# Where TensorE's operands start in SBUF: weights' parts 96 bytes into longer slots, the rest at multiples of 128

## The chip, the cores and the metric

The kernel runs on one core of a Trainium2 chip. The metric is device time in microseconds (us) from start to end of one execution; lower is better. The kernel before takes 298.7 us, the median of three runs (298.55 to 298.9). The profile comes from one more execution.

## What is computed

One transformer block on 256 tokens of 1,024 features, all in float32:

```python
u = rms_norm(h, mix_norm_g)
q, k, v, glu_a, glu_g = jnp.split(u @ w_in, splits, axis=-1)      # 512 columns each
attn_out = moba_attention(heads(q), heads(k), heads(v), rel_bias) # 8 heads of 64, causal, one block
conv_out = conformer_conv(glu_a, glu_g, conv_w, conv_b, conv_ln_g, conv_ln_b)  # 31 taps, LayerNorm, silu
h = h + jnp.concatenate([attn_out, conv_out], axis=-1) @ w_out
u = rms_norm(h, ffn_norm_g)
h = h + (jax.nn.silu(u @ w_gate) * (u @ w_up)) @ w_down           # 2,816 wide
return rms_norm(h, final_norm_g)
```

## The kernel before

**Products in three parts.** TensorE multiplies operands of type float32r. To keep float32's precision, each weight tile and each activation tile is split in two: an upper part (`wh`, `uh`), a copy rounded to float32r, and a lower part (`wl`, `ul`), the difference. A product is then three matmuls, wh by uh, wh by ul and wl by uh, added up in PSUM. ScalarE makes the upper parts of the weights and VectorE the lower ones, from raw tiles that SyncE's queue loads. The raw tiles have six slots, `wh` and `wl` nine each, of 128 x 1,024 floats; all weights of the kernel pass through the same slots.

**Two shapes.** A matmul has a stationary operand, 128 columns that a load of weights puts into the array, and a moving operand that streams through. In a and gate (`pa`, `pg`), queries and keys (`pqk`) and the output projection (`py`) the weights' parts are stationary and 256 columns of `u2` (or of the mixed activations `mh`, `ml`) move. In the values (`pv`), gate and up of the feed-forward (both `pf`) and down (`pd`, and `pe` at the very end) it is the other way round: the activations are stationary and 512 columns of weights move (256 in `pe`). A load of weights stands ahead of each matmul. Before this change and after it a and gate have 192 such matmuls, queries and keys 192, output 192, values 48, gate and up 528, down 252 and `pe` 24.

**What sets the order.** `PROGRAM`, a table written out by hand, gives the order of all steps up to the feed-forward; loops give it there. Each engine keeps to the program's order.

**Where the tiles lie.** The pools place their tiles one after another, each rounded up to 32 bytes per partition: first `const`, then `wts` (raw, `wh`, `wl`), then `w1`, which `w2` takes over for the feed-forward. The place where `const` starts is a multiple of 128. In the following a start is given as what is left of the byte address after division by 128. Before, `mhalf` (24 floats, 96 bytes) stands first, so `xs` and `u2` start at 96. `pv` is 16 floats longer than its data, which brings `ones` and `ident` to 0. The sums of squares and small tiles behind them bring `dg`, raw, `wh` and `wl` to 96, and `w2` as well (`fh`, `fl`). In `w1`, `accx` and `rbt` bring what follows to 0, `mh` and `ml` among it. Columns within tiles are cut at multiples of 128 bytes, except in the convolution. The pairs are thus, moving and stationary: a, gate, queries and keys 96 and 96; output 0 and 96; values, feed-forward and `pe` 96 and 96.

Of the kernel before, what the change touches and what calls it, by code (L numbers as in the profile page):

```python
# [10 lines left out]
F32 = mybir.dt.float32  # L11
F32R = mybir.dt.float32r
AF = mybir.ActivationFunctionType
ALU = mybir.AluOpType

P = 128
S = 256
D = 1024
KD = D // P
H = 8  # L20
HD = 64
NB = 32
TAPS = 31
CC = 4
# [6 lines left out]
ZN = 384  # L31
HW = 1024
# [4 lines left out]
FINE = ("a0_0", "a0_4")  # L37
COPY_V = (("a0_0", 0), ("a0_0", 1))
WARM = 9

PROGRAM = """
ld.a1_0 a0.0 pz a0.1 a0.2 a0.3 zs zd ld.a1_1 a0.4 a0.5 a0.6 a0.7 ld.qk0
# [13 lines left out]
PV_N = PV_FOLD + 32  # L56
# [3 lines left out]
def block_kernel(ctx, tc, xT, w_in, w_out, w_gu, w_down, pvec, gfin, relb, hot, out):  # L60
    nc = tc.nc
    const = ctx.enter_context(tc.tile_pool(name="const", bufs=1))
    wts = ctx.enter_context(tc.tile_pool(name="wts", bufs=9))
# [3 lines left out]
    w1 = ph1.enter_context(tc.tile_pool(name="w1", bufs=1))  # L67
# [3 lines left out]
    def mm(*args, **kw):  # L71
        return tc.keep_in_program_order(nc.tensor.matmul(*args, **kw))  # L72
# [12 lines left out]
    act, vec, pool, sync = (InOrder(e) for e in (nc.scalar, nc.vector, nc.gpsimd, nc.sync))  # L85

    def bank(i, name):
        return psum.tile([P, 512], F32, tag=f"b{i}", name=name)
# [17 lines left out]
    def pieces(name):  # L106
        n = HW // 2 if name in FINE else HW
        return [(i, slice(j, j + n)) for i in range(2) for j in range(0, HW, n)]
# [12 lines left out]
    def take(name):  # L121
        if name[0] in "gud" and name not in ("g0", "u0", "g1"):
            while order and len(raws) < 1 + LOOK:
                fetch(order[-1][2])
        return raws.pop(name)
# [5 lines left out]
    def high(name, i):  # L131
        if i == 0:
            raw = take(name)
            upper[name] = []
            parts[name] = []
            for n in range(2):
                wh = wts.tile([P, HW], F32R, tag="wh", name=f"wh_{name}_{n}")
                wl = wts.tile([P, HW], F32R, tag="wl", name=f"wl_{name}_{n}")
                parts[name].append((wh, wl))
                upper[name] += [(raw[n], wh, wl, c) for m, c in pieces(name) if m == n]  # L140
        raw, wh, wl, c = upper[name][i]
        if (name, i) in COPY_V:
            vec.tensor_copy(wh[:, c], raw[:, c])
        else:
            act.copy(wh[:, c], raw[:, c])
        made.add((name, i))
# [3 lines left out]
    def split(name, i=None):  # L150
        for n in range(len(pieces(name))) if i is None else (i,):
            if (name, n) not in made:
                high(name, n)
            raw, wh, wl, c = upper[name][n]
            vec.tensor_sub(wl[:, c], raw[:, c], wh[:, c].bitcast(F32))
# [10 lines left out]

    mhalf = const.tile([P, 24], F32, name="mhalf")
    xs = const.tile([P, KD, S], F32, name="xs")  # L170
    u2 = const.tile([P, KD, 2, S], F32R, name="u2")
    uh, ul = u2[:, :, 0], u2[:, :, 1]
    pv = const.tile([P, PV_N + 16], F32, name="pv")
    ones = const.tile([P, P], F32, name="ones")
    ident = const.tile([P, P], F32, name="ident")
    warm = const.tile([P, 1], F32, name="warm")
    accx = w1.tile([P, S], F32, name="accx")
    rbt = w1.tile([NB + 1, H], F32, name="rbt")
    hot_s = w1.tile([NB + 1, ZN], F32, name="hot_s", tag="lg", bufs=2)
    upad = [w1.tile([P, 2 * UW + 4], F32, name=f"upad{i}", tag="pts", bufs=4) for i in range(2)]  # L180
    ustk = []
    wstk = [w1.tile([P, 8 * Q, 32], F32, name=f"wstk{i}", tag="wstk", bufs=2) for i in range(2)]
    invc = w1.tile([P, P], F32, name="invc")
    vec.memset(warm, 0.0)
    act.dma_start(pv[:, 0:PV_T], pvec[:, 0:PV_T])
    act.activation(warm, warm, AF.Sigmoid)
# [3 lines left out]
        sync.dma_start(xs[:, k], xT[:, k * S : (k + 1) * S])  # L190
    pool.memset(ones, 1.0)
    pool.dma_start(hot_s, hot)
    pool.dma_start(rbt[0:NB, :], relb)
    wm = bank(4, "wm")
    for i in range(WARM):
        mm(wm[:, 0:P], ones, ones, start=i == 0, stop=i == WARM - 1)
    pool.memset(ident, 0.0)
    pool.affine_select(out=ident, in_=ident, compare_op=ALU.not_equal, fill=1.0, base=0,
                       pattern=[[-1, P]], channel_multiplier=1)
    pool.memset(mhalf, -0.5)  # L200
    pool.memset(rbt[NB : NB + 1, :], 1.0)
    for t in upad:
        pool.memset(t[:, 0 : TAPS - 1], 0.0)
        pool.memset(t[:, TAPS - 1 + S : UW + TAPS - 1], 0.0)
        pool.memset(t[:, UW + TAPS - 1 + S :], 0.0)
    pool.memset(invc, 1.0 / (CC * P))
    pool.dma_start(pv[:, PV_T:PV_N], pvec[:, PV_T:])

    col = lambda lo, i: pv[:, lo + i : lo + i + 1]
# [11 lines left out]
    def rstd(acc, n, eps, name, b):  # L221
        ps = bank(b, f"ps_{name}")
        for t in range(2):
            mm(ps[:, t : t + 1], acc[:, t * P : (t + 1) * P], ones[:, 0:1], start=True, stop=True)
        ms = const.tile([P, 2], F32, name=f"ms_{name}")
        vec.tensor_scalar(ms, ps[:, 0:2], 1.0 / n, eps, op0=ALU.mult, op1=ALU.add)
        rc = const.tile([P, 2], F32, name=f"rc_{name}")
        pool.tensor_tensor(rc, ms, mhalf[:, 0:2], op=ALU.pow)
        dg = const.tile([P, S], F32, name=f"dg_{name}", tag="dg")
        for t in range(2):  # L230
            vec.tensor_scalar(dg[:, t * P : (t + 1) * P], ident, rc[:, t : t + 1], None, op0=ALU.mult)
        return rc, dg

    def wide(dg, name, b):
        pb = bank(b, f"pb_{name}")
        mm(pb[:, :S], ones, dg, start=True, stop=True)
        return pb
# [22 lines left out]
    cv = lambda c: cacc[:, c]  # L260
# [75 lines left out]
    def scale_x():  # L336
        xn["c"], xn["d"] = rstd(accx, D, RMS_EPS, "x", 5)
# [16 lines left out]
    pzs = []  # L354

    def bias_mm():
        pzs.append(bank(6, "pz"))
        mm(pzs[0][0:H, 0:ZN], rbt, hot_s, start=True, stop=True)

    def bias_copy():  # L360
        act.copy(zs, pzs[0][0:H, 0:ZN])
# [120 lines left out]
    s4 = w1.tile([P, 2, S], F32, name="s4")  # L482
    ln = {}

    def norm(part):
        if part == 1:
            vec.tensor_add(s4[:, 0], s4[:, 0], s4[:, 1])
        elif part == 2:
            pm = bank(2, "pm")
            mm(pm[:, :S], invc, s4[:, 0], start=True, stop=True)  # L490
            for c in range(CC):
                vec.tensor_sub(cv(c), cv(c), pm[:, :S])
        elif part == 6:
            csq.append(w1.tile([P, CC, S], F32, name="csq", tag="wstk", bufs=2))
            for c in range(CC):
                act.activation(cw(c), cv(c), AF.Square)
        elif part == 3:
            vec.tensor_add(s4[:, 0], cw(0), cw(1))
            vec.tensor_add(s4[:, 1], cw(2), cw(3))
            vec.tensor_add(s4[:, 0], s4[:, 0], s4[:, 1])  # L500
        elif part == 7:
            _, ln["dg"] = rstd(s4[:, 0], CC * P, LN_EPS, "ln", 4)
        elif part == 4:
            ln["r"] = wide(ln["dg"], "ln", 5)
        else:
            for c in range(CC):
                vec.tensor_mul(cv(c), cv(c), ln["r"][:, :S])
                act.activation(cw(c), cv(c), AF.Silu, scale=col(PV_LG, c), bias=col(PV_LB, c))
                act.copy(mix[0][:, 4 + c], cw(c))
            for c in range(CC):  # L510
                vec.tensor_sub(mix[1][:, 4 + c], cw(c), mix[0][:, 4 + c].bitcast(F32))


    acch = const.tile([P, S], F32, name="acch")

    def finish(m):
        assert len(done) == KD - 3
# [7 lines left out]
    def a0(k):  # L525
        high(f"a0_{k // 4 * 4}", k % 4)
        upper_u(k, PV_G1)
        lower_u(k, PV_G1)
        split(f"a0_{k // 4 * 4}", k % 4)
        a_mm(0, k, f"a0_{k // 4 * 4}", k % 4 * 512)  # L530

    ops = {"ld": fetch, "zd": bias_out, "bd": bias_in, "ud": stack_out, "us": stack_in, "h": high, "w": split, "rb": row_scale, "pz": bias_mm, "zs": bias_copy, "vt": v_out, "rs": scale_x,
           "a0": a0, "a1": a1, "glu": glu, "qk": qk_mm, "qo": qk_out, "sc": score, "t": logits, "n": normed, "fl": flip,
           "fo": flip_out, "v": v_mm, "pv": pv_mm, "mo": mix_out, "l": norm, "o": o_mm, "f": finish, "c": conv,
           "co": conv_out, "cw": conv_weights, "ct": conv_taps, "hs": lambda m: sumsq(acch, xs[:, m], m, "h"),
           "sq": lambda k: sumsq(accx, xs[:, k], k, "x"), "g": lambda m: lower_u(m, PV_G2)}
# [96 lines left out]
    for k in range(KD):  # L633
        for t in range(2):
            up_mm(0, t, k)
        if k == 5:
            rc2, _ = rstd(acch, D, RMS_EPS, "h", next(spare))
            split("u1")
# [38 lines left out]
    a, b = FG - 2, FG - 1  # L677
    for t in range(2):
# [22 lines left out]
        ms = w2.tile([P, 2], F32, name=f"fms{t}")  # L701
        for n, (lo, hi) in enumerate(((512, 768), (768, 1024))):
# [5 lines left out]
            if n == 0:  # L708
# [4 lines left out]
                                 op0=ALU.mult, op1=ALU.add, accum_out=ms[:, 1:2])  # L713
# [97 lines left out]
```

## Time and profile before

| | us |
|---|---|
| median of three runs | 298.7 (298.55 to 298.9) |
| the profiled execution | 298.79 |
| its span, first to last instruction | 297.0 |
| TensorE busy with matmuls | 289.4 |
| loads of weights | 246.9 |
| VectorE busy | 203.9 |
| ScalarE busy | 149.7 |
| GpSimd busy | 44.3 |

A matmul's busy time begins when it starts and has a modelled end that overlaps the next one, so the means in the groups of the profile are no price of a matmul. What a matmul costs in a stream is the distance from start to start. The chain of work that ended last, in order of time, shows it directly: it takes each instruction from the end of the one before it, so that a piece's length divided by its count is the distance, apart from what enters at the piece's first instruction.

### The profile page before, as it was taken

To read this page: it belongs to the slowest core of one execution; us is meant where nothing else is said; L and a number is where in the kernel's file an instruction comes from. 1 tells how busy PE (TensorE), PEld (TensorE's weight loads), DVE (VectorE), ACT (ScalarE), POOL (GpSimd) and SP (SyncE) were. 2 spreads that over 40 slices of the span, in tenths; PEclk is the share of its full clock that TensorE was granted. 3 is DMA by queue.
4 is the path that set the end of the run, shared out by engine and by line. 5 is a ranking of instruction groups with operands and counts; after the bars stand their busy time and mean duration, and the time that the engine had idled before them with its cause. 6 is when DMAs were issued, how large, how long until landed. Compare 5 with 4: busy or idle time off the path is not lost.

```text
span 297.0 us, 4763 instructions
## 1 busy us (share of the span) xinstructions
PE 289.4 (97%) x1750; PEld 246.9 (83%) x1750; DVE 203.9 (69%) x373; ACT 149.7 (50%) x251; POOL 44.3 (15%) x83
## 2 busy tenths in 40 slices
PE   8999999999999999999999999999999999999991
PEld 7999986988689998888888888888888888888880
DVE  2877999888988688867875738291847456321884
ACT  2984564354583768826555445271717263402531
POOL 4000000000000000124131303320421313130000
PEclk9999999999999999999999999999999999999996
DMA  6999779936227445797997968979694959520012
GB/s 182 344 406 335 251 170 261 382 94 195 74 73 225 142 144 200 244 354 228 307 348 168 310 166 275 303 259 374 222 282 134 297 144 311 165 71 0 1 68 75
DMA packets 21624, 63.73 MB, mean 215 GB/s; under 512 B 3117, under 2 KB 5701, under 8 KB 21600
## 3 DMA queue, kind: packets, MB, share of 16 engines
q1 hardware_dynamic: 18176, 54.80, 57.2%
q0 software_dynamic: 2992, 8.08, 9.8%
q10 hardware_dynamic: 432, 0.54, 0.5%
q8 instruction: 14, 0.23, 0.3%
q14 instruction: 10, 0.08, 0.1%
HBM read 58.08 MB, written 5.32 MB: 213 GB/s over the span
## 4 chain that ended last, share of the span: by engine, by line
PE 92%; issue 2%; DMA 2%; DVE 1%; SPq 0%; POOLq 0%; POOL 0%; ACT 0%; DVEq 0%
PE pf L72 40%; PE pd L72 17%; PE pqk L72 8%; PE py L72 8%; PE pv L72 4%; PE pa L72 4%; PE pg L72 4%; PE pc L72 4%; DMA xs<-in_xT 2%; PE ps L72 1%; PE pt L75 1%; PE po L72 1%; DVE ht L83 1%; SPq L83 0%; DVE hg L83 0%
## 5 line engine op out<-in xcount | busy, mean ns | idle before, releaser
L72 PE MATMUL pf<-wh_u,u 128*128 128x512 f32 x176 | 56.2, 390 | 0.0
L72 PE MATMUL pf<-wh_g,u 128*128 128x512 f32 x176 | 55.9, 389 | 0.0
L83 DVE TENSOR_TENSOR ff<-fs,pf 128x256 f32<-128x256 f32 x22 | 9.1, 420 | 53.4 <-ACT fs L83 53.4
L83 ACT ACTIVATE fs<-pf,rc_h 128x256 f32<-128x256 f32 x22 | 10.4, 476 | 65.9 <-PE pf L72 65.4
L72 PEld LDWEIGHTS pf<-wh_u,u 128*128 128x128 f32 x176 | 33.0, 188 | 6.8
L72 PEld LDWEIGHTS pf<-wh_g,u 128*128 128x128 f32 x176 | 33.0, 188 | 6.8
L72 PE MATMUL pf<-wl_g,u 128*128 128x512 f32 x88 | 34.2, 389 | 0.0
L72 PE MATMUL pf<-wl_u,u 128*128 128x512 f32 x88 | 34.2, 389 | 0.0
L72 PE MATMUL pd<-wh_d,fh 128*128 128x512 f32 x84 | 32.9, 391 | 0.0
L72 PE MATMUL pd<-wh_d,fl 128*128 128x512 f32 x84 | 32.7, 390 | 0.0
L72 PE MATMUL pd<-wl_d,fh 128*128 128x512 f32 x84 | 32.7, 389 | 0.0
L83 DVE TENSOR_TENSOR wl_u<-raw_u,wh_u 128x1024 fp32r<-128x1024 f32 x22 | 26.6, 1223 | 7.5 <-ACT wh_u L83 7.4
L83 POOL DMA_DIRECT2D fb<-fd x40 | 23.2, 588 | 46.5 <-DMA fd<-fv 22.8
L83 ACT CAST wh_u<-raw_u 128x1024 fp32r<-128x1024 f32 x22 | 22.9, 1053 | 12.5 <-PE pf L72 9.2
L83 DVE TENSOR_TENSOR wl_g<-raw_g,wh_g 128x1024 fp32r<-128x1024 f32 x22 | 25.9, 1221 | 2.0 <-ACT wh_g L83 2.0
L83 DVE TENSOR_TENSOR wl_d<-raw_d,wh_d 128x1024 fp32r<-128x1024 f32 x22 | 25.6, 1205 | 0.5 <-ACT wh_d L83 0.5
L72 PE MATMUL pqk<-u,wh_qk 128*128 128x256 f32 x128 | 23.6, 286 | 0.0
L83 ACT CAST wh_g<-raw_g 128x1024 fp32r<-128x1024 f32 x22 | 22.0, 1049 | 0.0
L83 ACT CAST wh_d<-raw_d 128x1024 fp32r<-128x1024 f32 x22 | 21.9, 1045 | 0.0
L72 PEld LDWEIGHTS pqk<-u,wh_qk 128*128 128x128 f32 x128 | 20.0, 192 | 0.4 <-issue 0.3
L72 PEld LDWEIGHTS pf<-wl_u,u 128*128 128x128 f32 x88 | 16.5, 188 | 3.4
L72 PEld LDWEIGHTS pf<-wl_g,u 128*128 128x128 f32 x88 | 16.5, 188 | 3.4
(156 smaller groups left out, 558.4 us busy)
## 6 DMA issues: line engine op xcount, KB each, us to landing
raw_g<-in_w_gu SPq DMA_DIRECT2D x22, 512.0 KB, 5.6
raw_u<-in_w_gu SPq DMA_DIRECT2D x22, 512.0 KB, 7.0
raw_d<-in_w_down SPq DMA_DIRECT2D x22, 512.0 KB, 4.7
raw_qk<-in_w_in SPq DMA_DIRECT2D x8, 512.0 KB, 7.2
raw_o<-in_w_out SPq DMA_DIRECT2D x8, 512.0 KB, 4.2
fd<-fv POOLq DMA_DIRECT2D x10, 256.0 KB, 4.0
fb<-fd POOLq DMA_DIRECT2D x40, 64.0 KB, 5.8
ustk<-ud SPq DMA_DIRECT2D x8, 288.0 KB, 5.7
```

The source lines that it names most:

```text
L72: return tc.keep_in_program_order(nc.tensor.matmul(*args, **kw))
L75: return tc.keep_in_program_order(nc.tensor.transpose(o, i, ident))
L83: return lambda *a, **k: tc.keep_in_program_order(f(*a, **k))
```

## The change

The tiles are placed anew; no instruction is moved. The row of instructions of each engine is the same in order, with three differences: GpSimd's `memset` of `invc` is gone, the mean of the convolution's LayerNorm is a product with `ones` where it was one with `invc` (whose elements were 1/512), and VectorE's four subtractions of it are multiply-and-adds that bring in the -1/512.

- `wh` and `wl` have slots of 1,056 floats. The weights of a and gate (`a0`, `a1`), queries and keys (`qk`) and output (`o`) begin 24 floats into them; those of values, gate, up and down at the slot's start.
- `mhalf` stands behind `ident` and has 2 floats, `pv` is 8 floats shorter, and one tile `acc` in `const` serves as `accx` and as `acch`. `xs`, `u2`, `dg`, raw and the slots of `wh` and `wl` start at 0.
- `rbt` is 32 floats wide, of which 8 are used. `w1` and `w2` start at 0, and `mh`, `ml`, `fh` and `fl` lie at 0.

The pairs, moving and stationary, are now: a, gate, queries and keys 0 and 96; output 0 and 96, as before; values, feed-forward and `pe` 0 and 0.

```diff
+SHIFT = {"a": 24, "q": 24, "o": 24}
...
             for n in range(2):
-                wh = wts.tile([P, HW], F32R, tag="wh", name=f"wh_{name}_{n}")
-                wl = wts.tile([P, HW], F32R, tag="wl", name=f"wl_{name}_{n}")
+                s = SHIFT.get(name[0], 0)
+                wh, wl = (wts.tile([P, HW + 32], F32R, tag=w, name=f"{w}_{name}_{n}")[:, s : s + HW] for w in ("wh", "wl"))
                 parts[name].append((wh, wl))
...
-    mhalf = const.tile([P, 24], F32, name="mhalf")
+
     xs = const.tile([P, KD, S], F32, name="xs")
     u2 = const.tile([P, KD, 2, S], F32R, name="u2")
     uh, ul = u2[:, :, 0], u2[:, :, 1]
-    pv = const.tile([P, PV_N + 16], F32, name="pv")
+    pv = const.tile([P, PV_N + 8], F32, name="pv")
     ones = const.tile([P, P], F32, name="ones")
     ident = const.tile([P, P], F32, name="ident")
+    mhalf = const.tile([P, 2], F32, name="mhalf")
     warm = const.tile([P, 1], F32, name="warm")
-    accx = w1.tile([P, S], F32, name="accx")
-    rbt = w1.tile([NB + 1, H], F32, name="rbt")
+    accx = acch = const.tile([P, S], F32, name="acc")
+    rbt = w1.tile([NB + 1, 32], F32, name="rbt")
...
-    invc = w1.tile([P, P], F32, name="invc")
...
-    pool.memset(invc, 1.0 / (CC * P))
...
-            mm(pm[:, :S], invc, s4[:, 0], start=True, stop=True)
+            mm(pm[:, :S], ones, s4[:, 0], start=True, stop=True)
             for c in range(CC):
-                vec.tensor_sub(cv(c), cv(c), pm[:, :S])
+                vec.scalar_tensor_tensor(cv(c), pm[:, :S], -1.0 / (CC * P), cv(c), op0=ALU.mult, op1=ALU.add)
...
-    acch = const.tile([P, S], F32, name="acch")
```

## Rows read from the trace of the kernel before

**Rows 1.** The page: busy engines, TensorE's granted clock in 40 slices, chain by engine.

```profile
PE 289.4 (97%) x1750; PEld 246.9 (83%) x1750; DVE 203.9 (69%) x373; ACT 149.7 (50%) x251; POOL 44.3 (15%) x83
...
PEclk9999999999999999999999999999999999999996
...
PE 92%; issue 2%; DMA 2%; DVE 1%; SPq 0%; POOLq 0%; POOL 0%; ACT 0%; DVEq 0%
```

**Rows 2.** Waits of TensorE's weight loads, the longest: us in total, times, longest.

```profile
PEld wm L72 <- POOL ones L83: 1.0, 1, 1.0
PEld pa L72 <- ACT u L83: 0.8, 1, 0.8
PEld ps L72 <- DVE cacc L83: 0.8, 2, 0.4
```

**Rows 3.** The chain in order of time: start, length (us), engine, tile, line, count.

```profile
18.52 0.24 PE pg L72 x2
18.75 0.24 PE pa L72 x2
...
30.91 8.64 PE pqk L72 x72
...
54.11 2.88 PE pqk L72 x24
...
95.51 14.24 PE py L72 x120
...
142.91 5.44 PE pd L72 x24
148.35 10.88 PE pf L72 x48
```

**Rows 4.** Groups by shape, TensorE: count, busy us, mean ns, then idle before.

```profile
L72 PE MATMUL pf<-wh_g,u 128*128 128x512 f32 x176 | 55.9, 389 | 0.0
...
L72 PE MATMUL pd<-wh_d,fh 128*128 128x512 f32 x84 | 32.9, 391 | 0.0
...
L72 PE MATMUL pqk<-u,wh_qk 128*128 128x256 f32 x128 | 23.6, 286 | 0.0
...
L72 PE MATMUL pa<-u,wh_a 128*128 128x256 f32 x64 | 13.7, 295 | 0.1
...
L72 PE MATMUL pv<-wh_v,u 128*128 128x512 f32 x32 | 10.8, 399 | 0.0
```

**Rows 5.** Timeline of TensorE's matmuls, us 118.4 to 121, first and last rows.

```profile
118.45 0.39 PE L72 MATMUL pf<-wl_u,u 128*128 128x512 f32 x1
118.68 0.63 PE L72 MATMUL pf<-wh_u,u 128*128 128x512 f32 x2
...
120.53 0.39 PE L72 MATMUL pf<-wl_u,u 128*128 128x512 f32 x1
120.76 0.39 PE L72 MATMUL pf<-wh_u,u 128*128 128x512 f32 x1
```

**Rows 6.** Groups by shape, loads of float32 stationary operands that start at 0, 96 and 32.

```profile
L72 PEld LDWEIGHTS ps_ln<-ones,s 128*128 128x128 f32 x4 | 0.5, 190 | 0.0
L72 PEld LDWEIGHTS ps_x<-ones,accx 128*128 128x128 f32 x4 | 0.5, 190 | 0.2 <-DVE accx L83 0.2
L72 PEld LDWEIGHTS ps_h<-ones,acch 128*128 128x128 f32 x4 | 0.5, 190 | 0.2 <-DVE acch L83 0.2
```

**Rows 7.** Groups by shape, VectorE and GpSimd, around the LayerNorm's mean.

```profile
L83 DVE SCALAR_TENSOR_TENSOR ht<-pe,rc_h,ht 128x256 f32<-128x256 f32 x4 | 1.9, 483 | 0.2
...
L83 DVE TENSOR_TENSOR cacc<-cacc,pm 128x256 f32<-128x256 f32 x4 | 1.4, 417 | 0.2 <-PE pm L72 0.2
...
L83 POOL MEMSET invc<- 128x128 f32 x1 | 0.2, 210 | 0.0
```

**Rows 8.** Timeline of VectorE behind the mean's subtraction.

```profile
83.18 1.42 DVE L83 TENSOR_TENSOR cacc<-cacc,pm 128x256 f32<-128x256 f32 x4 [0.19 <-PE pm L72]
84.51 0.96 DVE L83 TENSOR_TENSOR ml<-po,mh 128x256 fp32r<-128x256 f32 x2
86.54 0.76 DVE L83 TENSOR_TENSOR ml<-po,mh 128x256 fp32r<-128x256 f32 x2 [1.07 <-ACT mh L83]
```

More of the change, by code (lines that the diff above doesn't have):

```diff
@@ L192, in block_kernel @@
     pool.dma_start(hot_s, hot)
-    pool.dma_start(rbt[0:NB, :], relb)
+    pool.dma_start(rbt[0:NB, 0:H], relb)
     wm = bank(4, "wm")
@@ L200, in block_kernel @@
     pool.memset(mhalf, -0.5)
-    pool.memset(rbt[NB : NB + 1, :], 1.0)
+    pool.memset(rbt[NB : NB + 1, 0:H], 1.0)
     for t in upad:
@@ L227, in rstd @@
         rc = const.tile([P, 2], F32, name=f"rc_{name}")
-        pool.tensor_tensor(rc, ms, mhalf[:, 0:2], op=ALU.pow)
+        pool.tensor_tensor(rc, ms, mhalf, op=ALU.pow)
         dg = const.tile([P, S], F32, name=f"dg_{name}", tag="dg")
@@ L357, in bias_mm @@
         pzs.append(bank(6, "pz"))
-        mm(pzs[0][0:H, 0:ZN], rbt, hot_s, start=True, stop=True)
+        mm(pzs[0][0:H, 0:ZN], rbt[:, 0:H], hot_s, start=True, stop=True)
     def bias_copy():
```

## The prediction, made before the result was seen

> **What bounds the kernel now.** The page comes first: TensorE is busy for 289.4 of 297.0 us, 92% of the chain that ended last lies on it, and its granted clock is at the upper of its two levels, 2.4 GHz, in every slice but the last, where it has no more matmuls [rows 1]. Then its waits: the loads of weights ahead of the matmuls stand still for 1.0 us at the very start, 0.8 us once more in the start for `u`, and 0.8 us in two pieces later [rows 2]. So the time is the number of matmuls times their distance, and every nanosecond per matmul is seen in the end, with nothing else late. That is why the chain in order of time is the view to read [rows 3]; busy means such as 286 or 389 ns [rows 4] contain modelled ends and are no distances.
>
> The distances fall into three classes, and here the start of the operands comes in.
> - 256 columns, moving at 96, stationary at 96: queries and keys take 8.64 us for 72, which is 120.0 ns; a burst of 24 takes 2.88 us, again 120.0; a and gate take 0.24 us for two [rows 3].
> - 256 columns, moving at 0, stationary at 96: output takes 14.24 us for 120, which is 118.67 ns [rows 3]. It is the only float32r stream of the kernel with different starts, and it is 1.33 ns faster although it does the same work.
> - 512 columns, 96 and 96: gate and up take 10.88 us for 48, down 5.44 us for 24, both 226.67 ns [rows 3].
>
> The step from 256 to 512 columns at 96 and 96 is 106.67 ns, exactly 256 columns at 2.4 GHz. What is left over, 13.33 ns, is the same for both widths, so it is a price per matmul and not per column, and it is the thing that a start could change. It is not always 13.33: behind an interruption 512-column matmuls are slower for a while. From 118.45 to 120.53 us stand nine distances (the rows with x2 hold two) in 2.08 us, 231.1 ns each, before the stream settles at the 226.67 that the long pieces show [rows 5, 3]. Which distance a stream settles at is therefore a state, and the change moves operands, so it can move that state in either direction.
>
> **The change part by part.**
>
> Queries, keys, a and gate go from 96 and 96 to 0 and 96, which is what output has. There are 192 + 192 matmuls; the first 24 of a and gate run in the start, where they wait for transfers, so 360 count. At the output's distance each saves 1.33 ns, 0.48 us in all; some fifty of them stand right behind interruptions, where the streams have not settled, and I take 0.45 us. Bounds: nothing if the output's 1.33 ns come from something else in that stream (0 us), and the whole 13.33 ns if the left-over went entirely (360 x 13.33 ns = 4.8 us). I take the output's value since it is the same width, type and pair of starts.
>
> Values, gate and up, and down go from 96 and 96 to 0 and 0: 48 + 528 + 252 = 828 matmuls of 512 columns, and 24 of 256 in `pe`. No float32r row has 0 and 0. The float32 loads whose stationary operand starts at 0, 96 and 32 take 190 ns each [rows 6], so the start of a stationary operand by itself costs nothing there; what distinguishes the output from queries and keys is then either the moving start alone or the difference of the two starts. By the difference, 0 and 0 is the same as 96 and 96 and nothing happens. By the moving start alone, each of the 828 saves what the output saves, 1.33 ns, 1.10 us in all. From above: the settled state is lost, and each stays at the 231.1 ns of rows 5, 4.44 ns more; about 60 of them are in that state anyway, so 765 x 4.44 ns = 3.4 us dearer. From below: the whole left-over goes, 828 x 13.33 ns = 11.0 us. I take zero, by the difference: the nearest row is gate and up itself, whose operands keep their position against each other.
>
> The mean of the LayerNorm: four multiply-and-adds on VectorE in place of four subtractions. One with an input in PSUM takes 483 ns against 417 [rows 7], together 0.26 us more. Behind them VectorE makes `ml` from 84.51 us and then idles 1.07 us, waiting for ScalarE [rows 8]; that idle time takes the 0.26 us in, and TensorE's waits name nothing there [rows 2]. Cost nothing; without the cover 0.26 us. The removed `memset` (0.21 us [rows 7]) was GpSimd's and nobody waited for it. `acc` as one tile makes the second sum of squares wait for reads of the first, which belongs to the start of the kernel: nothing.
>
> The transfers write raw tiles and `xs` at 0 instead of 96. In the start alone is anybody waiting for them, 0.8 us [rows 2]. No row has the same transfer at another start; it is worth at most those 0.8 us, as much the other way, and I take zero. Writes of VectorE and ScalarE at another start: no row shows a price, TensorE never waits for them in the feed-forward, zero.
>
> Sum: 297.0 - 0.45 = 296.55 us of span. The profiled execution has 1.79 us around its span (298.79) and lies 0.09 us over the median of the runs, so the time is 298.25, in round numbers **298.3 us**.
>
> **The rivals.**
>
> *The wide matmuls gain too (faster).* The moving start alone counts, and the 828 go at 1.33 ns less: 298.25 - 1.10 = 297.15 us. For it: output and queries differ in exactly that start. Against it: they differ in the difference as well. Its far end, with all 13.33 ns gone from the 828, is 287.2 us; against this end speaks that output, whose moving operand starts at 0 already, still pays 12.0 ns of the 13.33.
>
> The Trainium skill's "TensorE: Matmul & The Clock Gate", under "Back-to-back issue gap", gives N / 2.4 + 2.5 ns for a warm matmul alone, which would be 109 and 216 ns here, an estimate from that page. The trace disagrees at every start it has: 118.67, 120.0 and 226.67 [rows 3].
>
> *The settled state is lost (slower).* At 0 and 0 the wide streams stay at the distance they have behind an interruption, 231.1 ns. It decides from the first long piece of gate and up; the time is 298.25 + 3.4 = 301.65 us. For it: the slower state exists, in each burst behind an interruption [rows 5], and moving the operands helped output precisely by keeping it out of a settled 120.0; the same can happen to a stream that is better off settled. Against it: the two starts keep their difference.
>
> *Starts do nothing (no change).* What makes output faster is something else, its four banks or the place of `mh`, and all starts are alike: 298.7 us. For it: the float32 loads don't care [rows 6]. Against it: output is the one stream with another pair, and the one with another distance.
>
> The Trainium skill speaks for this rival: "SBUF — State Buffer", under "Specifications (TRN2)", has lines of 16 bytes, and 0 and 96 are both multiples of 16, so a read touches as many lines from either; its "Operand start alignment" says that its rule is about legality, not speed. The output's 118.67 against 120.0 [rows 3] is not explained by it.
>
> **How the numbers follow.** The forecast has 0.42, the wide gain 0.28 (of which 0.08 for ends well below 297), the lost state 0.18, no effect 0.12. The forecast's own range is 297.6 to 298.9 us, by the transfers of the start and by some 60 unsettled matmuls of 512 columns that may settle sooner or later (60 x 4.44 ns = 0.27 us). To hold 8 in 10 the range takes in the wide gain at 297.15 and the lost state at 301.65: 296.6 to 301.9 us; the far end of the gain is left out. A measurement of this kernel tells 0.2% (0.6 us) from no change. Below 298.1 lie the wide gain and about a quarter of the forecast's chance: faster 0.38. Within 0.2% lie the rest of the forecast and no effect: 0.43. Slower by more is the lost state and a little of the rest: 0.19.
>
> **What the profile after would show.** In the chain: queries and keys at about 118.7 ns (72 in 8.54 us), output unchanged, gate and up at 226.67 (48 in 10.88 us). Queries and keys at 120.0 would make the first term wrong; 48 of gate and up in 10.82 us or less would show the wide gain, in 11.09 the lost state. Any wait of TensorE's loads over 1 us outside the start would mean that I overlooked who becomes late.

## The result: slower, and only from the feed-forward on

The changed kernel takes 301.43 us (median, 301.04 to 302.82) where the kernel before took 298.8 us in the same session (298.55 to 299.65). The ratio is 1.0092, 95% interval 1.0066 to 1.0119. The forecast was 298.3 us; the time is that of the rival "the settled state is lost", which gave 301.65 us.

The page of the changed kernel, as in rows 1 (busy engines, granted clock in 40 slices, chain by engine):

```profile
span 299.3 us, 4761 instructions
...
PE 291.4 (97%) x1750; PEld 245.8 (82%) x1750; DVE 204.0 (68%) x373; ACT 149.1 (50%) x251; POOL 44.0 (15%) x82
...
PEclk9999999999999999999999999999999999999997
...
PE 92%; issue 2%; DMA 2%; DVE 1%; SPq 0%; POOLq 0%; POOL 0%; ACT 0%; DVEq 0%
```

TensorE bounds the kernel as before, at the upper of its two clock levels in all but the last slice. So the clock does not explain the loss, and neither does a new wait: the longest waits of the weight loads are those of rows 2, within 0.2 us.

```profile
PEld pa L74 <- ACT u L85: 1.0, 1, 1.0
...
PEld ps L74 <- DVE cacc L85: 0.8, 2, 0.4
```

The chain in order of time, to be read against rows 3 (start, length in us, engine, tile, line, count):

```profile
30.07 8.52 PE pqk L74 x72
...
53.06 2.81 PE pqk L74 x24
...
94.29 14.28 PE py L74 x120
108.57 8.31 PE pf L74 x36
117.22 25.04 PE pf L74 x108
142.27 5.58 PE pd L74 x24
147.85 11.11 PE pf L74 x48
158.95 5.57 PE pd L74 x24
164.52 11.09 PE pf L74 x48
...
258.95 5.57 PE pd L74 x24
```

Queries and keys fell from 120.0 to 118.3 ns (8.52 us for 72). Gate and up rose from 226.67 to 231.0-231.5 ns (11.09 or 11.11 us for 48), down to 232 (5.57 for 24). From 142.27 to 258.95 us lie seven rounds of 72 wide matmuls: 116.68 us for 504, 231.5 ns each.

The balance: the last piece of output ended at 95.51 + 14.24 = 109.75 us before [rows 3]; now the feed-forward begins at 108.57, 1.18 us earlier. The span ends 2.3 us later (299.3 against 297.0). So 3.48 us went in the feed-forward and behind it, 4.46 ns for each of its 780 wide matmuls. That they are unsettled, and not evenly slower, is seen in the timeline of single matmuls (start, busy us): the starts lie 0.23, 0.23, 0.24 and 0.23 us apart.

```profile
195.82 0.40 PE L74 MATMUL pd<-wl_d,fh 128*128 128x512 f32 x1
196.05 0.39 PE L74 MATMUL pd<-wh_d,fl 128*128 128x512 f32 x1
196.28 0.40 PE L74 MATMUL pd<-wh_d,fh 128*128 128x512 f32 x1
196.52 0.40 PE L74 MATMUL pd<-wl_d,fh 128*128 128x512 f32 x1
196.75 0.39 PE L74 MATMUL pd<-wh_d,fl 128*128 128x512 f32 x1
```

In the trace's nanoseconds such a stretch repeats distances of 230, 236 and 234. Elsewhere, as at the end of the piece from 181.15 to 192.27 us, there are runs of six or seven at 226 and 227: the stream finds the settled distance and loses it again. What the two stretches have different is said behind the second experiment.

### The profile page after: what moved, and what is told of

Same layout as the page of the kernel before. It is cut to its first block, busy times and chain, and to the rows that moved or that the text cites. A ratio compares the mean times of both kernels' runs of the same rounds, so it can differ in the third digit from the quotient of the medians.

```text
span 299.3 us, 4761 instructions
## 1 busy us (share of the span) xinstructions
PE 291.4 (97%) x1750; PEld 245.8 (82%) x1750; DVE 204.0 (68%) x373; ACT 149.1 (50%) x251; POOL 44.0 (15%) x82
## 4 chain that ended last, share of the span: by engine, by line
PE 92%; issue 2%; DMA 2%; DVE 1%; SPq 0%; POOLq 0%; POOL 0%; ACT 0%; DVEq 0%
PE pf L74 41%; PE pd L74 18%; PE py L74 8%; PE pqk L74 8%; PE pv L74 4%; PE pa L74 4%; PE pc L74 4%; PE pg L74 4%; DMA xs<-in_xT 2%; PE ps L74 1%; PE pt L77 1%; PE po L74 1%; DVE ht L85 1%; SPq L85 0%; DVE hg L85 0%
## 5 line engine op out<-in xcount | busy, mean ns | idle before, releaser
L74 PE MATMUL pf<-wh_u,u 128*128 128x512 f32 x176 | 56.9, 393 | 0.0
L74 PE MATMUL pf<-wh_g,u 128*128 128x512 f32 x176 | 56.7, 393 | 0.0
L74 PEld LDWEIGHTS pf<-wl_g,u 128*128 128x128 f32 x88 | 16.5, 188 | 3.7
L74 PEld LDWEIGHTS pf<-wl_u,u 128*128 128x128 f32 x88 | 16.5, 188 | 3.7
```

## The experiments

In the words of the sections ahead a start was what is left of an address after division by 128. That is too coarse here. From the built programs I took, for every float32r matmul, the **difference**: start of the moving operand less start of the stationary one, what is left after division by 256. Before, gate, up, down, values, queries, keys, a and gate had 0, and output 160. In the changed kernel a slot of 1,056 floats is 4,224 bytes, 16.5 times 256, so that neighbouring slots lie 128 apart in this measure. Feed-forward: 408 matmuls at 0 and 372 at 128. A, gate, queries, keys and output: mixed, 32 and 160.

**Every pair of starts, streams alone.** No transformer: bursts of 48 matmuls, wide then narrow (512 and 256 columns), float32r, a load of weights ahead of each, all 16 pairs of starts of 0, 32, 64 and 96 bytes, slots of 4,096.

```python
for m, s in PAIRS:          # floats: 0, 8, 16, 24 for moving and stationary
    rest(g)                 # two small float32 products
    wide(m, s, g)
...
```

> This kernel leaves the transformer out: it runs only TensorE streams of 48 float32r matmuls, first 16 of 512 moving columns, then 16 of 256, one for each pair of starts (moving, stationary) out of 0, 32, 64 and 96 bytes past a multiple of 128, with two small float32 matmuls between the streams, and copies an input to the output. Operand sequences are those of gate and up (wide) and of queries and keys (narrow); slots of weights are 4,096 bytes apart, and no other engine works meanwhile. Theory 'start': where the operands start within 128 bytes decides by itself; then the wide stream at (96, 96) settles at 226.7 ns and that at (0, 0) stays near 231.5 ns, as in the two traces. Theory 'slots': the 4,224-byte distance of the slots unsettles the streams, so that here, with 4,096, (0, 0) and (96, 96) both settle at 226.7. Theory 'difference' (that of the prediction): equal differences of the starts give equal distances, all four equal pairs alike. For the narrow streams: (96, 96) 120.0 and (0, 96) 118.7 by all three.

Measured distance in ns, mean of the last 24 of each burst, by difference. Pairs with the same difference agree within 0.05 ns, whatever the starts themselves.

| difference | 0 | 32 | 64 | 96 | -32 | -64 | -96 |
|---|---|---|---|---|---|---|---|
| wide | 226.67 | 233.33 | 228.88 | 233.33 | 233.33 | 233.33 | 234.17 |
| narrow | 120.0 | 116.67 | 117.75 | 120.0 | 118.33 | 117.75 | 117.38 |

0 and 0 is indeed the same as 96 and 96: neither operand's start counts by itself. And the two widths want different things: zero is the best of these for wide matmuls and the worst for narrow ones.

**Every difference in steps of 16.** The same streams, stationary operand at 0, moving one at 0 to 240 bytes.

```diff
-PAIRS = [(m, s) for m in (0, 8, 16, 24) for s in (0, 8, 16, 24)]
+PAIRS = [(m, 0) for m in range(0, 64, 4)]
```

> Again streams alone, without the transformer: the stationary operand starts at a multiple of 256, the moving one 0, 16, 32 and so on to 240 bytes past a multiple of 256, 48 matmuls of 512 columns and then 48 of 256 for each; slots 4,096 bytes apart. Theory 'difference within 256': the distance goes by the difference of the two starts modulo 256. Then wide: 226.67 ns at 0, about 228.9 at 64, 233 to 234 at 32, 96, 160, 192 and 224, as in the streams before, and over 230 at 128, which has the same start modulo 128 as 0. Narrow: 120.0 at 0, 116.7 at 32, 117.75 at 64 and 192, 118.3 at 224. Theory 'difference within 128': 128 is the same as 0 in both, 226.67 and 120.0, and the loss with longer slots has another cause.

| difference | 0 | 16 | 32 | 48 | 64 | 80 | 96 | 112 |
|---|---|---|---|---|---|---|---|---|
| wide | 226.67 | 231.67 | 233.33 | 233.33 | 228.88 | 231.08 | 233.33 | 226.67 |
| narrow | 120.0 | 118.71 | 116.67 | 118.33 | 117.75 | 120.0 | 120.0 | 113.33 |

| difference | 128 | 144 | 160 | 176 | 192 | 208 | 224 | 240 |
|---|---|---|---|---|---|---|---|---|
| wide | 232.08 | 233.33 | 234.17 | 233.33 | 233.33 | 234.58 | 233.33 | 236.67 |
| narrow | 118.83 | 118.54 | 117.42 | 119.21 | 113.33 | 119.17 | 118.33 | 116.92 |

128 is not 0: nearly half of the changed kernel's wide matmuls have it, and a stream of it alone goes at 232.08 ns. That is not the whole loss. If the others had kept 226.67 ns, 372 x 5.41 ns = 2.0 us would be lost, and 3.48 are. With each start of the trace set beside its matmul's difference, the matmuls at 0 are seen to lose as much: interruptions left out, the next start follows after 231.1 ns on average behind a matmul of the feed-forward at 0 and after 231.6 behind one at 128. The repeated 236, 234 and 230 ns above go with differences that repeat 0, 128, 0: 236 from 0 to 128, 234 from 128 to 0, 230 from 0 to 0. The seven distances of 226 and 227 before 192.1 us lie behind seven matmuls at 0, which follow five more at 0. This speaks for the change of difference from one matmul to the next keeping a stream unsettled, at 0 too; a stream that alternates was not run alone.

The timeline gives whole bursts, here for wide at 0, 112 and 128 and for narrow at 0 and 112 (start, us from the first start to the last end, count):

```profile
9.97 11.52 PE L28 MATMUL b<-w,u 128*128 128x512 f32 x48
...
91.19 11.13 PE L28 MATMUL b<-w,u 128*128 128x512 f32 x48
...
102.52 11.40 PE L28 MATMUL b<-w,u 128*128 128x512 f32 x48
...
195.87 6.00 PE L28 MATMUL b<-u,w 128*128 128x256 f32 x48
...
238.91 5.74 PE L28 MATMUL b<-u,w 128*128 128x256 f32 x48
```

At 0 the wide burst is the longest of the three, 11.52 us, but that is no price of 0: it is the first burst of the kernel, with two long distances at its start (573 and 356 ns), and from the fourth distance on it goes at 226.67. In the run before, the later bursts at 0 take 11.13 to 11.18 us and settle after one to ten matmuls; at 112 it is one, and the same distance. At 128 the burst does not settle within its 48. One point disagrees with the run before: narrow at 192 (-64) gave 113.33 here and 117.75 there, so what a narrow stream settles at also depends on how it came in.

**The long slots alone.** The kernel before, with slots of 1,056 floats, every part at its slot's start, and, for room, the shared `acc` and the mean by `ones`. All starts are as before modulo 128.

```diff
-                wh = wts.tile([P, HW], F32R, tag="wh", name=f"wh_{name}_{n}")
-                wl = wts.tile([P, HW], F32R, tag="wl", name=f"wl_{name}_{n}")
+                wh = wts.tile([P, HW + 32], F32R, tag="wh", name=f"wh_{name}_{n}")[:, 0:HW]
+                wl = wts.tile([P, HW + 32], F32R, tag="wl", name=f"wl_{name}_{n}")[:, 0:HW]
...
```

> The kernel before with slots of 1,056 floats for the weights' parts, but every part still at the slot's start, so that all pairs of starts modulo 128 are those of the kernel before (the shared accumulator and the product with ones come along, to make room). Theory 'start': the streams of 512 columns keep 226.67 ns, 48 of gate and up in 10.88 us, time 298.8 us, ratio 1.000. Theory 'slots': they go to about 231.5 ns as in the changed kernel, 48 in 11.1 us, and without the gain of queries and keys the time is about 302 us, ratio 1.011.

302.42 us, ratio 1.0114 (1.0088 to 1.0139). Its chain shows the changed kernel's pieces:

```profile
143.68 5.58 PE pd L72 x24
149.25 11.11 PE pf L72 x48
160.36 5.57 PE pd L72 x24
165.93 11.09 PE pf L72 x48
```

5.58, 11.11, 5.57, 11.09: to the digit what the changed kernel has, though here u and the weights stand where they stood modulo 128. From the start of the feed-forward's first matmul to that of the last (`pe`) it is 184.0 us in both kernels, against 180.6 before. The length of the slots makes the loss, with no shift of any part.

**No shift, short slots.** The changed kernel with slots of 1,024 floats and nothing shifted, so that u, `mh` and all weights have difference 0. Everything else of the change stays.

```diff
-SHIFT = {"a": 24, "q": 24, "o": 24}
+SHIFT = {}
...
-... wts.tile([P, HW + 32], F32R, tag=w, name=f"{w}_{name}_{n}")[:, s : s + HW] ...
+... wts.tile([P, HW], F32R, tag=w, name=f"{w}_{name}_{n}")[:, s : s + HW] ...
```

> The changed kernel with slots of 1,024 floats and no shift, so that every float32r operand starts at a multiple of 128 and slots are 4,096 bytes apart. Theory 'start': the wide streams, at 0 and 0, stay near 231.5 ns (48 of gate and up in 11.1 us), time 301.5 us or a little more, ratio 1.009 to 1.012, according to what the narrow ones do at 0 and 0. Theory 'slots' and theory 'difference': 226.67 ns, narrow ones at 120.0 as at 96 and 96, output at 120.0 too, time 299.0 us, ratio 1.001.

299.17 us, ratio 1.0008 (0.9988 to 1.0028).

```profile
30.73 8.64 PE pqk L74 x72
...
95.32 14.38 PE py L74 x120
...
142.87 5.44 PE pd L74 x24
148.31 10.88 PE pf L74 x48
```

The loss is gone: 226.67 ns for wide, at starts of 0 modulo 128, and 180.6 us from the feed-forward's first matmul to the last. So are the gains: queries and keys are back at 120.0, and output, now at difference 0 too, rose from 14.24 to 14.38 us and settles at 120.0. The output's 1.33 ns before were its difference of 160, not its moving start. The rest of the change (the mean by multiply-and-add, the one `acc`, transfers to other starts) costs nothing that can be seen.

**u moved alone.** The kernel before with `mhalf` behind `u2` instead of ahead of it, which puts `xs` and `u2` 96 bytes lower. Difference of the feed-forward's gate and up and of the values 96, of a, gate, queries and keys 160, of down 0 as before.

```diff
-    mhalf = const.tile([P, 24], F32, name="mhalf")
     u2 = const.tile([P, KD, 2, S], F32R, name="u2")
+    mhalf = const.tile([P, 24], F32, name="mhalf")
```

> The kernel before with one line moved: the 24 floats of mhalf stand behind xs and u2 instead of ahead of them. u2 then starts at 0 and everything behind it stays at 96: a, gate, queries and keys 0 and 96, values and gate and up 96 and 0, down 96 and 96 as before; slots 4,096 bytes apart. Theory 'start', if the moving operand's start is what counts: the wide streams stay at 226.67 ns, a, gate, queries and keys gain 1.33 ns each, time 298.35 us, ratio 0.9985. Theory 'start', if the stationary operand's counts: gate and up 231.5 ns, 528 x 4.8 ns = 2.5 us, time 300.9, ratio 1.007, down unchanged at 226.67. Theory 'difference': gate and up lose their settled state as their difference changes, 300.9 us as well; theory 'slots': 298.35 us.

302.34 us, ratio 1.0116 (1.0091 to 1.0141).

```profile
143.62 5.47 PE pd L72 x24
149.09 11.20 PE pf L72 x48
```

Gate and up: 11.20 us for 48, 233.3 ns, the streams' value for 96. Down, in the same kernel, settles at 226.67 within each 24 (5.47 us, 0.03 for the way there). The weights are in the same slots in both, and of the operands of TensorE's float32r matmuls only u has moved, which is gate and up's stationary operand: the moving start alone cannot be what counts. The theory 'difference' had the direction, and 300.9 us was too low, because it took 231.5 ns for a difference that costs 233.3: 528 x 6.67 ns is 3.5 us and not 2.5.

**Only the narrow matmuls off zero.** The kernel before with u 32 bytes further until the feed-forward, and `accx` 32 floats longer, which moves `mh` and `ml`. Differences: a, gate, queries, keys and output 32, feed-forward 0.

```diff
-    u2 = const.tile([P, KD, 2, S], F32R, name="u2")
+    u2 = const.tile([P, KD * 2 * S + 64], F32R, name="u2")
+    at = lambda lo: u2[:, lo : lo + KD * 2 * S].rearrange("p (k l s) -> p k l s", k=KD, l=2)
+    u_in, u_ff = at(8), at(0)
...
-    accx = w1.tile([P, S], F32, name="accx")
+    accx = w1.tile([P, S + 32], F32, name="accx")[:, 0:S]
...
```

> The kernel before with its slots; u2 is 64 floats longer, and before the feed-forward its data lie 8 floats further in (a difference of 32 for a, gate, queries and keys, and of 224 for values), in the feed-forward at the start (difference 0); the sum of squares is 32 floats longer, which brings mh and ml to a difference of 32 too. Theory 'difference within 256', by the streams alone: narrow matmuls at 116.67 ns, 360 x 3.33 = 1.2 us less for a, gate, queries and keys, 192 x 2.0 = 0.4 us less for output, values 48 x 3 ns = 0.15 us more; gate and up and down stay at 226.67. Time 297.5 us, ratio 0.995. By 'difference within 128' the same narrow gain. By 'start' (the operand's own start counts) no gain: ratio 1.000.

298.17 us against 298.74, ratio 0.9968 (0.9956 to 0.9981): faster, by 0.3%.

```profile
30.11 8.47 PE pqk L72 x72
...
94.25 14.13 PE py L72 x120
...
141.51 5.44 PE pd L72 x24
146.95 10.88 PE pf L72 x48
```

Queries and keys settle at 116.67 ns in the trace, the streams' value for 32, and so does output in its first two pieces, of 48 and 24; in its long piece it settles at 117.75 (14.13 us for 120). The wide matmuls keep 226.67. This is the narrow gain without the wide loss, reached by moving the small operand instead of the weights' slots. The gain is somewhat smaller than the ratio of 0.995 that the distances gave; the long piece of output, and the way to the settled distance in each burst, are part of what is missing.

**Longer slots in whole steps of 256.** The changed kernel with slots of 1,088 floats (4,352 bytes, 17 times 256). The room is made with one slot for the squares of the norm instead of three, and three for the small `mn` instead of four.

```diff
-... wts.tile([P, HW + 32], F32R, tag=w, name=f"{w}_{name}_{n}")[:, s : s + HW] ...
+... wts.tile([P, HW + 64], F32R, tag=w, name=f"{w}_{name}_{n}")[:, s : s + HW] ...
-            sq = const.tile([P, S], F32, name=f"sq_{n}{k}", tag="sq", bufs=3)
+            sq = const.tile([P, S], F32, name=f"sq_{n}{k}", tag="sq", bufs=1)
```

> The changed kernel with slots of 1,088 floats, 17 x 256 bytes, in place of 1,056, so that the difference of the starts is the same in every slot also modulo 256 (0 for values and the feed-forward, 160 for a, gate, queries, keys and output). To make room, two slots of squares and one of small tiles are given up. Theory 'difference within 256': the wide streams settle at 226.67 ns again, queries and keys go at about 118.7 as output does in the kernel before, time 298.5 us, ratio about 0.9985; that is what was predicted for the change. Theory 'any longer slot': about 301.5 us, ratio 1.009.

304.71 us, ratio 1.0211 (1.0191 to 1.0232): the expected time was missed by far. Chain and waits (of the weight loads, then of ScalarE) show why:

```profile
97.36 14.10 PE py L74 x120
...
146.89 5.44 PE pd L74 x24
152.33 10.88 PE pf L74 x48
```

```profile
PEld ps_x L74 <- DVE acc L85: 2.8, 1, 2.8
PEld ps_h L74 <- DVE acc L85: 2.4, 1, 2.4
```

```profile
ACT sq_x L85 <- DVE acc L85: 3.4, 4, 1.3
```

The streams did what was expected, 226.67 ns in the whole feed-forward. The time went elsewhere: with one slot for the squares, ScalarE's next square waits for VectorE's sum of the last (3.4 us in four waits, all new), and TensorE waits 2.8 and 2.4 us for the two norms' sums; before, that wait was 0.2 us each [rows 6]. These waits are read from the profiled execution, the fastest, of 302.87 us; the four others took 304.68 to 305.82 us with a mean granted clock of 0.984 to 0.986 against its 0.995, and where they lost the rest isn't shown. So this run says nothing of what the change would be worth with such slots. It does settle the measure: its wide differences are 0 and 256 modulo 512 in about equal parts, and both stand at 226.67. Whole steps of 256 count for nothing in the wide matmuls, half a step does.

**The best difference of the streams, 112.** As the run with 32, with u 28 floats further and `mh` and `ml` 20 floats into longer tiles, which makes 112 of all narrow differences.

```diff
-    u_in, u_ff = at(8), at(0)
+    u_in, u_ff = at(28), at(0)
...
-... w1.tile([P, KD, S], F32R, name=n, tag="stk", bufs=2) ...
+... w1.tile([P, KD * S + 64], F32R, name=n, tag="stk", bufs=2)[:, 20 : 20 + KD * S].rearrange("p (k s) -> p k s", k=KD) ...
```

> The kernel before, with u made 28 floats (112 bytes) further than the feed-forward's u until the feed-forward begins, and mh and ml 20 floats into longer slots. Differences of moving start and stationary start, modulo 256: a, gate, queries, keys and output 112, values 144, gate, up and down of the feed-forward 0 as before. Theory (the difference modulo 256 sets the distance, in the kernel as in the streams alone): queries, keys and output at 113.33 ns, values at 233.3, the feed-forward settled at 226.67. 360 x 6.67 + 192 x 5.33 - 48 x 6.67 = 3.1 us less than before: span 293.9, time 295.7, ratio 0.990. Rival 1 (what helps is any difference other than zero, 116.7 ns being what can be had, and 113.33 a chance state of the streams alone): as with difference 32, 298.2 us, ratio 0.997. Rival 2 (113.33 is lost at each interruption, as a settled state, and the bursts of 24 never reach it): queries and keys between 114 and 117, time between 296 and 298.

297.59 us against 298.94, ratio 0.9951 (0.9932 to 0.997): faster, and less so than expected. The chain (the page's shares by engine first) and the waits of the weight loads:

```profile
PE 80%; DVE 6%; DMA 4%; ACT 3%; issue 3%; SPq 1%; POOL 0%; POOLq 0%; DVEq 0%
```

```profile
4.50 5.86 DMA raw_a<-in_w_in
10.37 6.45 DMA raw_a<-in_w_in
...
29.10 1.05 DVE gl L83 x3
...
32.71 2.35 DVE wl_qk L83 x2
...
96.24 13.63 PE py L72 x120
...
148.49 10.88 PE pf L72 x48
```

```profile
PEld pc L72 <- DVE rs L83: 1.2, 1, 1.2
...
PEld ps_x L72 <- DVE accx L83: 0.8, 1, 0.8
```

The distance is there: output takes 13.63 us for 120, 113.6 ns, and the trace shows 113 and 114 in queries, keys, a and gate once they have settled, which takes up to a dozen matmuls behind an interruption. The time lies where rival 2 put it, but the bursts of 24 do reach 113.33. What rival 2 had no word of is the front: up to 44 us the chain no longer runs on TensorE. It begins with the transfers of `raw_a`, up to 16.8 us, passes through ScalarE's squares and upper parts and then through VectorE's lower parts `wl_qk`, and the loads wait 1.2 us for the convolution's `rs`, a wait that rows 2 do not have, and 0.8 us for `accx`, where it was 0.2 [rows 6]. Of the profiled execution's narrow gain before the convolution (264 x 6.67 ns = 1.8 us) nothing is left, and the first `pc` starts 1.2 us later than before (44.63 against 43.40 us); behind it, from the first `pc` to the feed-forward, 65.1 us stand against 66.2. The faster matmuls need not be the cause of all of it: with the long slots alone, where queries and keys were hardly faster (8.58 us for 72), the profiled execution's chain also begins with `raw_a`'s transfers, and `ps_x` waits 0.7 us for its sum. The execution shown here took 298.94 us, near the upper end of this kernel's 296.41 to 299.03; how much of the front is lost in the others isn't settled.

## Why the prediction was wrong, step by step

**What bounds the kernel: right.** TensorE's distances set the time, no wait appeared, and every nanosecond per matmul was seen in the end.

**The narrow term: right in direction and, for queries and keys, in size.** Forecast 8.54 us for 72, measured 8.52. The reason was only half right: their difference is not output's 160 but a mixture of 32 and 160, because the slots alternate. All in all 1.18 us were gained by the start of the feed-forward where 0.45 were forecast. Of it 0.20 is no gain of distances: the first long stretch of a and gate began at 7.58 instead of 7.78 us, in one execution of each kernel. Another 0.43 lies between there and the norm's sum behind it: the 132 matmuls' distances fell from 121.9 to 119.75 ns on average, 0.28 us, and the sum follows 0.14 us closer. The other 0.55 lies in the pieces from there to the feed-forward.

**The wide term: wrong, and this is the step that failed.** "By the difference, 0 and 0 is the same as 96 and 96 and nothing happens ... I take zero, by the difference." The rule was right, as the 16 pairs show; its use was wrong. The pairs were written down modulo 128, a measure which nothing in the trace supported and which I took over from the section on where the tiles lie. In it the slots' 4,224 bytes are 33 whole units and vanish. The slots' length stood in the section on the change, and I costed it at nothing by not costing it at all. The zero should have carried the question what else a longer slot moves: every second slot of `wh` and of `wl` against u. With it, the difference of nearly half the wide matmuls was new, and no row had a price for it. What the runs show in place of the zero is 3.48 us, or 4.46 ns for each of the 780 wide matmuls of the feed-forward: with the long slots alone they stand at 231.5 ns, with short ones at 226.67.

**The rival that happened was priced well, for another reason than it gave.** The lost state was put at 231.1 ns, from nine distances behind an interruption [rows 5], and at 3.4 us; measured are 231.5 ns and 3.48 us. It decided where the rival said, from the first long pieces of gate and up, and the sign named for it, 48 in 11.09 us, is in the chain. What spoke against it, "the two starts keep their difference", was false for 372 of 780. But the rival lost the settled state at 0 and 0, where the streams alone and the run without shift settle at 226.67. That a stream thrown out again and again goes at nearly the distance of one behind an interruption was not worked out by anyone; that the two prices agree so closely is in part luck.

**The wide gain and "starts do nothing": both fall.** With all starts at 0 modulo 128 and short slots the wide matmuls are at 226.67 as before, and starts move both widths.

**The small terms: right.** The mean's multiply-and-adds, `acc` and the transfers cost nothing: the run without shift and long slots has them all and stands at 1.0008. That is clear to some 0.3%, its interval being 0.9988 to 1.0028. VectorE's idle time behind the mean is 1.07 us still in the changed kernel, as in rows 8:

```profile
82.00 1.42 DVE L85 SCALAR_TENSOR_TENSOR cacc<-pm,cacc 128x256 f32<-128x256 f32 x4
83.34 0.96 DVE L85 TENSOR_TENSOR ml<-po,mh 128x256 fp32r<-128x256 f32 x2
85.36 0.76 DVE L85 TENSOR_TENSOR ml<-po,mh 128x256 fp32r<-128x256 f32 x2 [1.07 <-ACT mh L85]
```

The four take 1.42 us together, as the subtractions did, so even the 0.26 us were not to be seen.

## What to carry to other kernels

When operands move, write down for each stream the difference of its two starts in the finest measure that the trace can't exclude, slot by slot, and not for one slot: a tile that grows shifts all its neighbours. A stream's distance can be had for little by moving the small operand that it shares instead of the slots that all streams share. And what a stream gains is worth its price only while what feeds it is in time: in the profiled execution of the run with 112, transfers, ScalarE and VectorE set the pace in the front of the kernel, and the gain of that part was not seen.

## What the runs showed of the hardware

- The distance of float32r matmuls, with a load of weights ahead of each, depends on the difference of the operands' starts modulo 256 bytes: 226.67 to 236.67 ns for 512 columns, 113.33 to 120.0 for 256. Zero gave the shortest for 512 columns, as did 112, and the longest for 256, as did 80 and 96; 112 gave the shortest for both.
- For 256 columns the difference does not settle it alone. The same difference has stood at two distances: 192 at 117.75 and 113.33 ns (the two runs of streams), 160 at 117.4 (streams) and 118.67 (output before), 32 at 116.67 and 117.75 (output's pieces in one kernel). What decides between them, the runs don't show.
- At most differences there is no single distance but a cycle, such as 238, 231, 231 ns for 512 columns at 96. Where the difference changes from one matmul to the next, as in the changed kernel, matmuls at 0 go slower too: 231.1 ns on average instead of 226.67.
- So the moving operand's read and the load of a stationary one are not free of each other; whether it is the load of the same matmul or that of the next isn't shown. "TensorE: Matmul & The Clock Gate" of the Trainium skill, under "Step-by-step: what each phase is for", gives TensorE two independent read ports and says that loading the next weights takes no read bandwidth from the running matmul. The measurement goes against that here: a stream of unchanged moving operands went from 226.67 to 233.3 ns when only the stationary one moved (gate and up in the run with u moved alone). What the two reads share, the runs don't show.
